# A two-layer attention and mixture-of-experts kernel on one core: next layer's tiles interleaved with a quarter's down weights, and the GpSimd share of the splits moved to ScalarE and VectorE

## The chip, the cores and the metric

The kernel runs on one core of a Trainium2 chip. The metric is the device time of one execution in microseconds (us). Engines are named as the profile names them: PE is TensorE, ACT is ScalarE, DVE is VectorE, POOL is GpSimd, SP is SyncE, whose queue here does nothing but issue transfers from HBM.

## What is computed

Two layers over 256 tokens of width 1024, then a last RMS norm. Each layer mixes the tokens in three ways (latent attention, stick-breaking attention with a soft plus, causal pooling), projects back, and adds a mixture of 32 experts with two experts chosen per token:

```python
def hybrid_layer(x, ...):
    hn = rms_norm(x, norm1_g)
    proj = jnp.einsum('bsd,df->bsf', hn, w_in)
    ya = mla_mixer(proj[..., :o1], proj[..., o1:o2], proj[..., o2:o3], ...)
    yb = stick_breaking_mixer(qkv_b[:, :, 0], qkv_b[:, :, 1], qkv_b[:, :, 2])
    yc = pool_mixer(proj[..., o4:], pool_w, pool_scale)
    x = x + jnp.einsum('bsm,md->bsd', jnp.concatenate([ya, yb, yc], -1), w_out)
    return x + hier_moe(rms_norm(x, norm2_g), ...)

# stick breaking: strict is the mask of earlier positions
log_1m_beta = jnp.where(strict, -jax.nn.softplus(z), 0.0)
between = lax.cumsum(log_1m_beta, axis=3, reverse=True) - log_1m_beta
a = jnp.where(strict, jnp.exp(jax.nn.log_sigmoid(z) + between), 0.0)

# experts
a, b = einsum('nd,edf->nef', t, w_gate[g]), einsum('nd,edf->nef', t, w_up[g])
y = y + einsum('nef,efd->nd', silu(a) * b * combine[:, g, :, None], w_down[g])
```

Everything is float32. The expert weights alone are some 200 MB, so the traffic from HBM is the larger part of the work.

## The kernel before, in words

**Storage.** `Ring` (L43) holds 25 slots of 1 MB in SBUF: 12 pairs and one single. All weights pass through them, in the fixed order of a list, `stream`, that `Net.__init__` fills (L229 to L259). A rehearsal of the program (`rehearsed`, L126) finds, for each entry of the list, the first moment in the program at which a slot is free. SP issues the transfers one after the other in the list's order; an issue waits until the last reader of its slot is done, and all that follow in the list wait behind it. Entries are named by tile: `wa`, `wqk`, `wvu` are the parts of the input projection (0.8 to 1 MB each, two of each per layer), `sm`, `uq`, `wo` are other mixer weights, `wh` are gate and up weights of the experts, `ww` and `wt` their down weights. `wt` holds the down weights of six of the eight expert groups, cut in four quarters of the output columns; one entry of 2 MB has a quarter's weights of two groups.

**Exact products in two parts.** The input projection, the latent projections and the output projection multiply each operand as a high part (rounded to the reduced format fp32r) and a low part (the rest), in three matmuls (`mm3`, L312). `parts` (L318) makes the two: the high part by a copy, the low part by a subtraction of it. `weights` (L327) lists the pieces of the mixer weights, each 128 x 512 or 128 x 416, and `split` (L348) makes the parts of the next piece into one of four buffers, four pieces ahead of PE. In the kernel before, a piece with an even number has its high part from ACT and its low part from DVE. A piece with an odd number has its high part from DVE (a cast) and its low part from POOL, unless its last argument `how` forbids it (the first quarter of layer 0, `sm` and `uq`). 38 pieces go the odd way. In the stick-breaking part, `stick_parts` (L590) makes the parts of the soft plus, 128 x 768 at a time, twice in each layer: high from ACT, low from POOL.

**Stages of a layer.** `mixers` (L523) runs the value projections (`values_in`), the attention scores `z` of the stick-breaking heads, the soft plus of them (Abs, Exp, Ln on ACT, L578 to L582, then L584 on DVE), the latents (`latents` L477, `rescale` L493), the query projection, and at L673 `breaks`, the last reader of the soft plus's parts `sH` and `sL`. `route` chooses experts. `experts` (L912) goes through eight groups, then through the four quarters of the output columns (L1016). In a quarter each of the six groups has: `down` (16 matmuls with `wt`), `parts` of the result (a copy on ACT, a subtraction on DVE), one step of the next layer's input projection (`next(beside)`, L1033), and `scatter` (4 matmuls back to the tokens). The steps beside the second quarter (q = 1) are two with `wa`, two with `wqk`, two with `wvu`, all of the next layer's first tiles; beside the first quarter there are none, since the new x is not yet there. `arrive` (L403) transposes the quarter of x that has just become final and makes its parts.

Each engine works in the order in which its instructions are written. The order around the change is thus the order of `stream` for SP, and the order of calls of `split`, `parts` and `stick_parts` for ACT, DVE and POOL.

Of the kernel before, what the change touches and what calls it, by code (L numbers as in the profile page):

```python
# [9 lines left out]
F32 = mybir.dt.float32  # L10
# [4 lines left out]
OP = mybir.AluOpType  # L15
AX = mybir.AxisListType

L, S, D = 2, 256, 1024
# [9 lines left out]
SM_UK, SM_UV, SM_PW, SM_RT = 0, 512, 1024, 1280  # L28
# [166 lines left out]
class Net:  # L195
    def __init__(self, tc, ctx, a, plan):
# [20 lines left out]
        def w(l, k, *idx, then=()):  # L217
            for i in idx:
                add(f"{k}{i}.{l}", a[k][l, i], *then)
# [13 lines left out]
        for l in range(L):  # L233
            w(l, "wvu", *range(min(l, 1), 2))
            add(f"sm.{l}", a["small"][l])
            add(f"uq.{l}", a["uq"][l])
            w(l, "wo", 3, 2, 0, 1)
            for g in range(8):
                for i in range(0, 12 if g < 8 - TAIL else 8, 2):
                    src = a["wh"][(l * 8 + g) * 4 + i // 2] if i < 8 else a["ww"][(l * (8 - TAIL) + g) * 2 + i // 2 - 4]  # L240
                    add(f"we{g * 12 + i}.{l} we{g * 12 + i + 1}.{l}", src)
            for q in range(4):
                if l + 1 == L:
                    if q == 1:
                        add("fg", a["fg"])
                elif q < 3:
                    w(l + 1, ("wa", "wqk", "wa")[q], q // 2)
                    if q == 1:
                        w(l + 1, "wvu", 0)
                else:  # L250
                    w(l + 1, "wqk", 1)
                for p in range(TAIL // 2):
                    names = [f"we{(8 - TAIL + 2 * p + i) * 12 + 8 + q}.{l}" for i in range(2)]
                    src = tails(l, q, p)
                    if (l, q, p) == (L - 1, 3, TAIL // 2 - 1):
                        for i in range(2):
                            add(names[i], src[:, i * 2048:i * 2048 + 2048])
                    else:
                        add(" ".join(names), src)  # L259

        c = lambda n, *s, dt=F32: cst.tile([128, *s], dt, name=n)
# [22 lines left out]
        for i, n in ((0, 4), (8, 32)):  # L284
            k = min(i, 4)
# [29 lines left out]
        self.mm(out, a[0], b[1], False, False)  # L315
        self.mm(out, a[1], b[0], False, stop)

    def parts(self, hi, lo, in_, scale=None, pool=False):  # L318

        V = self.nc.gpsimd if pool else self.nc.vector  # L320
        self.ev("v" if pool else "a", hi, in_, scale)
        if scale is None:
            V.tensor_tensor(lo, in_, hi.bitcast(F32), op=OP.subtract)  # L323
        else:
            V.scalar_tensor_tensor(lo, in_, scale, hi.bitcast(F32), op0=OP.mult, op1=OP.subtract)  # L325

    def weights(self, l):  # L327

        add = lambda name, c, n, last, how=0: self.feed.append((f"{name}.{l}", c, n, last, how))
        for q in range(4):  # L330
            for name, n in (("wa", 416), ("wqk", 512)):
                for k in (2 * q, 2 * q + 1):
                    add(f"{name}{k // 4}", k % 4 * n, n, k % 4 == 3, l + q == 0)
            for k in range(2 * q, 2 * q + 2) if l and q < 2 else ():
                add(f"wvu{k // 4}", k % 4 * 512, 512, k % 4 == 3)
        for k in range(4 if l else 0, 8):
            add(f"wvu{k // 4}", k % 4 * 512, 512, k % 4 == 3)
        add("sm", SM_UK, 512, False, 1)
        add("sm", SM_UV, 512, False, 1)
        for j in range(4):  # L340
            add("uq", j * 512, 512, j == 3, 1)
        for c in (6, 7, 4, 5, 0, 1, 2, 3):
            for n in range(2):
                add(f"wo{c // 2}", c % 2 * 1024 + n * 512, 512, c % 2 + n == 2)
        self.wbuf = [v3(t, 4, 512) for t in self.ring.two("wHL")]
        self.turns = 0

    def split(self, ahead=AHEAD):  # L348

        while self.feed and len(self.ready) <= ahead:  # L350
            name, c, n, last, how = self.feed.popleft()
            piece = self.ring.get(name)[:, c:c + n]
            hl = [b[:, self.turns % 4, 0:n] for b in self.wbuf]
            self.parts(*hl, piece, pool=self.turns % 2 and not how)
            self.turns += 1
            self.ready.append(hl)
            if last:
                self.ring.drop(name)
# [164 lines left out]
    def mixers(self, l):  # L523
        nc, ps, ring, vec = self.nc, self.ps, self.ring, self.vec
        sm, mm, mm3, ev, tr = self.sm, self.mm, self.mm3, self.ev, self.tr
        V, A, G = nc.vector, nc.scalar, nc.gpsimd
# [32 lines left out]
        sp, dT = v3(spare, 4, 384), v3(spare, 2, 256, 1536)  # L559
# [15 lines left out]
        for h in (0, 2):  # L575
            hs = slice(h, h + 2)
# [11 lines left out]
        sH, sL = (v3(t, 4, 384) for t in ring.two("sHL"))  # L588

        def stick_parts(h):  # L590
            hs = slice(h, h + 2)
            A.activation(sH[:, hs], sp[:, hs], AF.Copy)
            G.tensor_tensor(sL[:, hs], sp[:, hs], sH[:, hs].bitcast(F32), op=OP.subtract)

        for t in range(2):
            ev("av"[t], vu[:, t], ps[:, 6 + t], r1[:, t:t + 1])
# [2 lines left out]
        w = self.weight()  # L599
        for j in range(2):  # L600
            b = ps[:, 4 + j]
            for e in range(2):
                c = (2 * j + e) * 128
# [4 lines left out]
        w = self.weight()  # L608
# [633 lines left out]
```

## Time and profile before

| | us |
|---|---|
| median of 3 runs (609.23, 611.42, 611.27) | 611.27 |
| the profiled execution | 609.29 |
| its span | 607.7 |
| PE busy in the span | 525.3 (86%) |
| DVE, ACT, POOL busy | 255.2, 146.3, 93.5 |
| SP's transfers (227.33 MB), share of the 16 DMA engines' time | 91.2% |

The span runs from the first to the last instruction of the profiled execution, and 1.6 us of its time lie outside. Busy time is the union of the instructions of an engine. PE's is no measure of its peak, since matmuls overlap and their ends are modelled. The transfers are busy for most of the span, so the times at which they are not are the ones to look for.

### The profile page before, as it was taken

How to read it: one execution, taken by the hardware profiler on the slowest of the kernel's cores; microseconds unless marked ns; L12 is line 12 of the kernel's file. 1: busy time of each engine (PE TensorE's matmuls, PEld its weight loads, DVE VectorE, ACT ScalarE, POOL GpSimd, SP SyncE). 2: the span in 40 equal slices, each digit the busy share in tenths (PEclk: the TensorE clock that was granted, in tenths of full speed). 3: DMA queues.
4: the chain of work that ended last, by engine and by line, in shares of the span. 5: the costliest groups of instructions: out<-in, count | busy, mean ns of one | idle time of the engine just before them, and what ended most of it. 6: DMA issues, size and time to landing. Idle time of an engine off the chain costs nothing. (4 is left out here: it accounts for less than half of the span.)

```text
span 607.7 us, 10429 instructions
## 1 busy us (share of the span) xinstructions
PE 525.3 (86%) x4232; PEld 342.2 (56%) x4232; DVE 255.2 (42%) x640; ACT 146.3 (24%) x351; POOL 93.5 (15%) x138
## 2 busy tenths in 40 slices
PE   8989999898886887769997799998898578889983
PEld 7968877554341543446766597774254325435652
DVE  4879765432320222143337686663332212212322
ACT  4465543200000001122223844422000000012212
POOL 2534323000000000011212332310000000100001
PEclk9999999999997899879999899999999879998998
DMA  8999778999999999999999729879999999999992
GB/s 300 399 424 397 258 297 293 369 387 424 424 427 424 426 427 426 425 423 428 427 418 428 306 63 355 313 304 386 385 422 428 424 424 428 425 426 428 426 386 77
DMA packets 25407, 228.72 MB, mean 376 GB/s; under 512 B 2817, under 2 KB 5121, under 8 KB 6914
## 3 DMA queue, kind: packets, MB, share of 16 engines
q1 hardware_dynamic: 24914, 227.33, 91.2%
q8 instruction: 37, 0.61, 0.4%
q10 hardware_dynamic: 432, 0.59, 0.3%
q14 instruction: 24, 0.20, 0.1%
HBM read 226.85 MB, written 1.05 MB: 375 GB/s over the span
## 5 line engine op out<-in xcount | busy, mean ns | idle before, releaser
L305 PE MATMUL ps<-pair,pair 128*32 128x256 f32 (+7 forms) x3152 | 385.6, 440 | 56.1 <-DVE pair L893 20.2
L305 PEld LDWEIGHTS ps<-pair,pair 128*32 128x32 f32 (+2 forms) x3152 | 226.8, 143 | 181.6 <-issue 102.9
L305 PE MATMUL ps<-pair 128*128 128x256 f32 (+7 forms) x416 | 78.3, 364 | 4.6 <-DVE pair L893 3.5
L371 ACT ACTIVATE pair<-ps 128x256 fp32r<-128x256 f32 (+5 forms) x82 | 36.8, 451 | 147.2 <-PE ps L305 133.8
L305 PEld LDWEIGHTS ps<-pair 128*128 128x128 f32 (+3 forms) x416 | 49.8, 182 | 32.8 <-issue 15.8
L323 DVE TENSOR_TENSOR pair<-ps,pair 128x256 fp32r<-128x256 f32 (+1 forms) x58 | 25.1, 433 | 86.5 <-ACT pair L371 86.5
L323 POOL TENSOR_TENSOR pair<-pair,pair 128x512 fp32r<-128x512 f32 (+1 forms) x33 | 43.8, 1327 | 93.2 <-DVE pair L373 60.4
L946 DVE TENSOR_REDUCE ws<-ps 128x1 f32<-128x256 f32 x16 | 6.8, 425 | 121.8 <-PE ps L365 121.8
L943 ACT ACTIVATE pair<-ps 128x256 f32<-128x256 f32 x16 | 6.1, 384 | 207.4 <-PE ps L305 193.4
L323 DVE TENSOR_TENSOR pair<-pair,pair 128x512 fp32r<-128x512 f32 (+1 forms) x47 | 44.6, 951 | 14.4 <-ACT pair L371 13.8
L922 POOL TENSOR_TENSOR pair<-pair,comb 128x128 f32<-128x128 f32 x32 | 12.2, 401 | 235.6 <-PE ps L305 223.2
L906 DVE TENSOR_TENSOR pair<-ps,vec 128x512 f32<-128x512 f32 x32 | 22.1, 691 | 49.5 <-PE ps L305 49.3
L371 ACT ACTIVATE pair<-pair 128x512 fp32r<-128x512 f32 (+1 forms) x47 | 28.9, 619 | 15.2 <-PE ps L305 10.3
L365 PE MATMUL ps<-ident,pair 128*128 128x128 f32 x128 | 23.3, 286 | 5.0 <-DVE pair L948 2.9
L373 DVE COPY pair<-ps 128x512 f32<-128x512 f32 (+3 forms) x25 | 17.1, 689 | 23.7 <-PE ps L305 15.4
L365 PEld LDWEIGHTS ps<-ident,pair 128*128 128x128 f32 x128 | 14.4, 141 | 22.3 <-issue 13.8
L305 PE MATMUL ps<-ident,ones 128*128 128x128 f32 x140 | 23.9, 303 | 1.6 <-POOL ident L274 1.6
L305 PEld LDWEIGHTS ps<-ident,ones 128*128 128x128 f32 x140 | 20.2, 210 | 3.6 <-issue 2.0
L325 DVE SCALAR_TENSOR_TENSOR pair<-ps,vec,pair 128x256 fp32r<-128x256 f32 x26 | 12.4, 482 | 19.1 <-ACT pair L371 19.1
L371 ACT ACTIVATE pair<-ps,vec 128x256 fp32r<-128x256 f32 x26 | 12.1, 474 | 27.2 <-PE ps L365 12.2
L641 ACT ACTIVATE pair<-pair,low 128x128 f32<-128x128 f32 (+1 forms) x32 | 14.1, 446 | 9.3 <-DVE low L635 9.3
L323 POOL TENSOR_TENSOR pair<-one,pair 128x416 fp32r<-128x416 f32 (+1 forms) x5 | 6.1, 1217 | 55.6 <-DVE pair L373 55.6
(143 smaller groups left out, 333.9 us busy)
## 6 DMA issues: line engine op xcount, KB each, us to landing
pair<-in_wh SPq DMA_DIRECT2D x39, 2048.0 KB, 19.1
pair<-in_wh SPq DMA_DIRECT2D x47, 1024.0 KB, 11.2
pair<-in_wt SPq DMA_DIRECT2D x23, 2048.0 KB, 32.3
pair<-in_ww SPq DMA_DIRECT2D x11, 1024.0 KB, 7.4
pair<-in_wo SPq DMA_DIRECT2D x8, 1024.0 KB, 18.1
pair<-in_ww SPq DMA_DIRECT2D x2, 2048.0 KB, 8.1
pair<-in_wqk SPq DMA_DIRECT2D x3, 1024.0 KB, 33.5
pair<-in_wvu SPq DMA_DIRECT2D x3, 1024.0 KB, 11.5
```

The lines of the kernel that those rows point to most:

```text
L305: self.nc.tensor.matmul(out, lhsT, rhs, start=start, stop=stop, skip_group_check=True)
L323: V.tensor_tensor(lo, in_, hi.bitcast(F32), op=OP.subtract)
L325: V.scalar_tensor_tensor(lo, in_, scale, hi.bitcast(F32), op0=OP.mult, op1=OP.subtract)
L365: self.nc.tensor.transpose(out, in_, self.ident)
L371: nc.scalar.activation(out, in_, AF.Copy, scale=1.0 if scale is None else scale)
L373: nc.vector.tensor_copy(out, in_)
L641: A.activation(s[:, c], s[:, c], AF.Exp, scale=-1.0, bias=low[:, h, j:j + 1], accum_out=sums[:, h, j:j + 1])
L906: self.nc.vector.tensor_tensor(xs[:, 4 * n:4 * n + 4], v3(self.ps[:, b0 + n], 4, 128), self.vec[:, l, 8 + 4 * n:12 + 4 * n, None].to_broad ...
L922: G.tensor_tensor(d4, d4, comb[:, t, 4 * g:4 * g + 4, None].to_broadcast([128, 4, 32]), op=OP.mult)
L943: A.activation(h, ps[:, 2, 0:256], AF.Silu)
L946: V.tensor_reduce(ws, ps[:, 3, 256:512], axis=AX.X, op=OP.add)
```

## The change

In layer 0's tail, the second quarter's entries of the stream stood as `wqk0`, `wvu0`, `wt`, `wt`, `wt`. They now stand as `wt`, `wqk0`, `wt`, `wvu0`, `wt`. And POOL makes no parts any more: of all pieces of weights, and of the soft plus, ACT makes the high part and DVE the low part.

```diff
@@ -244,12 +244,13 @@
                 elif q < 3:
-                    w(l + 1, ("wa", "wqk", "wa")[q], q // 2)
-                    if q == 1:
-                        w(l + 1, "wvu", 0)
+                    if q != 1:
+                        w(l + 1, "wa", q // 2)
                 else:
                     w(l + 1, "wqk", 1)
                 for p in range(TAIL // 2):
+                    if l + 1 < L and q == 1 and p:
+                        w(l + 1, ("wqk", "wvu")[p - 1], 0)
                     names = [f"we{(8 - TAIL + 2 * p + i) * 12 + 8 + q}.{l}" for i in range(2)]
@@ -315,10 +316,10 @@
-    def parts(self, hi, lo, in_, scale=None, pool=False):
+    def parts(self, hi, lo, in_, scale=None):
 
-        V = self.nc.gpsimd if pool else self.nc.vector
-        self.ev("v" if pool else "a", hi, in_, scale)
+        V = self.nc.vector
+        self.ev("a", hi, in_, scale)
@@ -348,10 +349,10 @@
             hl = [b[:, self.turns % 4, 0:n] for b in self.wbuf]
-            self.parts(*hl, piece, pool=self.turns % 2 and not how)
+            self.parts(*hl, piece)
@@ -590,7 +591,7 @@
             A.activation(sH[:, hs], sp[:, hs], AF.Copy)
-            G.tensor_tensor(sL[:, hs], sp[:, hs], sH[:, hs].bitcast(F32), op=OP.subtract)
+            V.tensor_tensor(sL[:, hs], sp[:, hs], sH[:, hs].bitcast(F32), op=OP.subtract)
```

The rest of the diff takes the argument `how` out of `weights`. The new code has one line more from L247 on, so its L324 is the old L323.

SP's queue at the second quarter of layer 0's tail, before (a number behind `pair` tells the tile):

```order
L93 DMA pair_95<-in_wqk 128x2048
L93 DMA pair_971<-in_wvu 128x2048
L75 DMA pair_121<-in_wt 128x4096
L75 DMA pair_123<-in_wt 128x4096
L75 DMA pair_125<-in_wt 128x4096
L93 DMA pair_95<-in_wa 128x1664
```

and now:

```order
L75 DMA pair_971<-in_wt 128x4096
L93 DMA pair_95<-in_wqk 128x2048
L75 DMA pair_123<-in_wt 128x4096
L93 DMA pair_121<-in_wvu 128x2048
L75 DMA pair_125<-in_wt 128x4096
L93 DMA pair_95<-in_wa 128x1664
```

The same 8 MB, with the first 2 MB of down weights moved ahead of the two tiles; two of the tiles have changed places in the ring. No other row of SP's queue changes its order.

ACT at the same place, from the parts of the quarter of x that has arrived (`pair_2450`) on; `pair_1315` are the parts of a group's result, `pair_2451` the parts of weights. Before:

```order
L371 ACTIVATE pair_2450<-ps,vec 128x256
L380 ACTIVATE pair_127,ss<-x 128x256
L371 ACTIVATE pair_1315<-ps 128x256
L371 ACTIVATE pair_2451<-pair_95 128x512
L371 ACTIVATE pair_1315<-ps 128x256
L371 ACTIVATE pair_2451<-pair_971 128x512
L371 ACTIVATE pair_1315<-ps 128x256 x2
```

and now:

```order
L372 ACTIVATE pair_2450<-ps,vec 128x256
L381 ACTIVATE pair_127,ss<-x 128x256
L372 ACTIVATE pair_1315<-ps 128x256
L372 ACTIVATE pair_2451<-one 128x416
L372 ACTIVATE pair_2451<-pair_95 128x512 x2
L372 ACTIVATE pair_1315<-ps 128x256
L372 ACTIVATE pair_2451<-pair_121 128x512
L372 ACTIVATE pair_1315<-ps 128x256
L372 ACTIVATE pair_2451<-pair_121 128x512
L372 ACTIVATE pair_1315<-ps 128x256
```

Every piece now has its high part here, so the first piece of `wvu0` (`pair_121`) stands between the parts of the second and the third group's results, as it did before, and the second one behind the third's.

DVE in layer 0, from the evacuation of the projections (L375) to the query projection's (L620); `pair_149` are the parts of weights. Before:

```order
L375 TENSOR_SCALAR pair_95<-ps,r_320 128x512
L323 TENSOR_TENSOR pair_149<-pair_113,pair_149 128x512
L373 COPY pair_95<-ps 64x2x256 x2
L323 TENSOR_TENSOR pair_149<-pair_113,pair_149 128x512
L373 COPY pair_95<-ps 128x512
L323 TENSOR_TENSOR pair_149<-pair_113,pair_149 128x512
L620 TENSOR_TENSOR pair_110<-ps,tq 128x512
L323 TENSOR_TENSOR pair_149<-pair_113,pair_149 128x512
L620 TENSOR_TENSOR pair_110<-ps,tq 128x512
L373 CAST pair_149<-pair_113 128x512
L620 TENSOR_TENSOR pair_110<-ps,tq 128x512
```

and now:

```order
L376 TENSOR_SCALAR pair_95<-ps,r_320 128x512
L324 TENSOR_TENSOR pair_149<-pair_113,pair_149 128x512
L374 COPY pair_95<-ps 64x2x256 x2
L594 TENSOR_TENSOR pair_148<-pair_119,pair_148 128x768
L324 TENSOR_TENSOR pair_149<-pair_113,pair_149 128x512
L374 COPY pair_95<-ps 128x512
L324 TENSOR_TENSOR pair_149<-pair_113,pair_149 128x512
L621 TENSOR_TENSOR pair_110<-ps,tq 128x512
L324 TENSOR_TENSOR pair_149<-pair_113,pair_149 128x512
L621 TENSOR_TENSOR pair_110<-ps,tq 128x512
L594 TENSOR_TENSOR pair_148<-pair_119,pair_148 128x768
L324 TENSOR_TENSOR pair_149<-pair_113,pair_149 128x512
```

The two subtractions of the soft plus (L594) have come to DVE, and a cast has become a subtraction.

## Rows read from the trace of the kernel before

**Rows 1.** Busy time by stretches: stretch, its length, engines, PEclk, DMA share, GB/s.

```profile
54.00:64.00 10.00, 9.30 (x85) 8.80 (x84) 9.62 (x22) 3.25 (x11) 3.13 (x2) 1.00 0.57 239
260.00:270.00 10.00, 5.59 (x44) 3.55 (x45) 4.38 (x9) 2.40 (x8) 1.82 (x2) 0.66 1.00 427
347.00:360.60 13.60, 13.60 (x109) 12.85 (x109) 12.92 (x26) 6.76 (x16) 5.07 (x4) 0.91 0.00 0
398.00:594.00 196.00, 170.63 (x1543) 94.81 (x1546) 56.42 (x151) 22.63 (x52) 10.73 (x26) 0.96 0.98 408
```

**Rows 2.** SP's waits, 0 to 130 us, then 330 to 412: total, times, longest.

```profile
SPq L75 <- PE ps L305: 67.1, 12, 31.4
...
SPq L75 <- PE ps L305: 56.8, 8, 33.7
```

**Rows 3.** Timeline of SP's issues: start, length, what was issued.

```profile
63.88 4.86 SPq L75 DMA_DIRECT2D pair<-in_ww  x3
...
360.59 0.81 SPq L75 DMA_DIRECT2D pair<-in_ww  x2
```

**Rows 4.** Timeline of PE, 255 to 366 us; in brackets idle time before and its releaser.

```profile
258.84 0.66 PE L365 MATMUL ps<-ident,x 128*128 128x128 f32 x4 [0.84 <-DVE x L1045]
264.41 3.88 PE L305 MATMUL ps<-pair,pair 128*32 128x256 f32 x22 [4.92 <-DMA pair<-in_wt]
...
268.68 2.40 PE L305 MATMUL ps<-pair,pair 128*32 128x256 f32 x22
...
274.01 0.64 PE L305 MATMUL ps<-pair 128*128 128x256 f32 x4
...
345.53 9.16 PE L305 MATMUL ps<-pair,pair 128*128 128x512 f32 x54 [3.86 <-ACT pair L371]
```

**Rows 5.** Timeline of SP, the third `wt` entry of the second quarter.

```profile
239.13 0.33 SPq L75 DMA_DIRECT2D pair<-in_wt  x1
```

**Rows 6.** DMA issues of 239.0 to 239.5 us: KB, us from issue to landing.

```profile
pair<-in_wt SPq DMA_DIRECT2D x1, 2048.0 KB, 35.0
```

**Rows 7.** Timeline of PE in layer 0, 33 to 57 us.

```profile
33.32 1.23 PE L365 MATMUL ps<-ident,pair 128*128 128x128 f32 x8 [1.17 <-DVE pair L503]
...
42.20 0.50 PE L305 MATMUL ps<-pair,pair 128*128 128x512 f32 x1 [0.45 <-DVE pair L373]
43.93 11.88 PE L305 MATMUL ps<-pair,pair 128*128 128x512 f32 x73 [1.23 <-POOL pair L323]
56.50 2.77 PE L305 MATMUL ps<-pair,pair 128*128 128x256 f32 x18 [0.70 <-DVE pair L323]
```

**Rows 8.** Timelines of DVE and POOL at places where both work.

```profile
30.80 1.25 DVE L496 TENSOR_TENSOR s<-s,r 128x4 f32<-128x4 f32 x1 [0.38 <-POOL s L487]
...
30.73 1.30 POOL L323 TENSOR_TENSOR pair<-pair,pair 128x512 fp32r<-128x512 f32 x1
...
325.19 0.16 DVE L433 TENSOR_TENSOR rr<-rr,widths 128x4 f32<-128x4 f32 x1
...
351.99 2.13 DVE L323 TENSOR_TENSOR pair<-pair,pair 128x512 fp32r<-128x512 f32 x1
...
351.73 1.85 POOL L593 TENSOR_TENSOR pair<-one,pair 128x768 fp32r<-128x768 f32 x1 [2.12 <-ACT pair L592]
...
44.83 0.89 DVE L323 TENSOR_TENSOR pair<-pair,pair 128x512 fp32r<-128x512 f32 x1
```

**Rows 9.** Timelines of ACT and DVE in layer 0, 37 to 48 us.

```profile
37.62 0.84 ACT L371 ACTIVATE pair<-ps,vec 128x256 fp32r<-128x256 f32 x2 [3.23 <-POOL pair L323]
...
41.30 0.62 ACT L371 ACTIVATE pair<-pair 128x512 fp32r<-128x512 f32 x1
...
47.71 0.69 ACT L371 ACTIVATE pair<-ps,r 128x512 f32<-128x512 f32 x1 [0.33 <-PE ps L305]
...
41.74 0.41 DVE L373 CAST pair<-pair 128x512 fp32r<-128x512 f32 x1
42.07 0.68 DVE L323 TENSOR_TENSOR pair<-pair,pair 128x512 fp32r<-128x512 f32 x1
```

More of the change, by code (lines that the diff above doesn't have):

```diff
@@ L327, in weights @@
     def weights(self, l):
-        add = lambda name, c, n, last, how=0: self.feed.append((f"{name}.{l}", c, n, last, how))
+        add = lambda name, c, n, last: self.feed.append((f"{name}.{l}", c, n, last))
         for q in range(4):
@@ L332, in weights @@
                 for k in (2 * q, 2 * q + 1):
-                    add(f"{name}{k // 4}", k % 4 * n, n, k % 4 == 3, l + q == 0)
+                    add(f"{name}{k // 4}", k % 4 * n, n, k % 4 == 3)
             for k in range(2 * q, 2 * q + 2) if l and q < 2 else ():
@@ L337, in weights @@
             add(f"wvu{k // 4}", k % 4 * 512, 512, k % 4 == 3)
-        add("sm", SM_UK, 512, False, 1)
-        add("sm", SM_UV, 512, False, 1)
+        add("sm", SM_UK, 512, False)
+        add("sm", SM_UV, 512, False)
         for j in range(4):
-            add("uq", j * 512, 512, j == 3, 1)
+            add("uq", j * 512, 512, j == 3)
         for c in (6, 7, 4, 5, 0, 1, 2, 3):
@@ L350, in split @@
         while self.feed and len(self.ready) <= ahead:
-            name, c, n, last, how = self.feed.popleft()
+            name, c, n, last = self.feed.popleft()
             piece = self.ring.get(name)[:, c:c + n]
             hl = [b[:, self.turns % 4, 0:n] for b in self.wbuf]
-            self.parts(*hl, piece, pool=self.turns % 2 and not how)
+            self.parts(*hl, piece)
             self.turns += 1
```

## The prediction, made before the changed kernel was run

> **What bounds the kernel now.** I first read the busy time by stretches [rows 1]. From 398 to 594 us the transfers are busy for 0.98 of the time at 408 GB/s, so the end is set by the moment at which this last run of transfers starts. Between 347.0 and 360.6 us they move nothing, and PE is busy throughout; from 54 to 64 us, at the same place in layer 0, they run at 239 GB/s. SP's waits say why [rows 2]: its longest waits in both layers, 31.4 and 33.7 us, are ended by PE matmuls. The issues that end them, at 63.88 and 360.59 [rows 3], are of `ww` entries whose slots held the soft plus's parts, and the last matmuls that read those are the ones of `breaks`. So the ring is full, transfers stop, and they go on when PE has come to the end of `breaks`. How much is loaded before each hole is fixed by the ring and by the order of `stream`. Whatever lets PE reach `breaks` earlier in layer 0 or layer 1 makes the hole shorter and moves everything behind it; the two gains add up.
>
> What makes PE late? In layer 1 the row at 264.41 shows it [rows 4]: the quarter before is done with its transposes at 258.84 + 0.66 = 259.5, and the second quarter's first group waits 4.92 us for its down weights. From there to 322 us PE runs almost without idle time; the two later quarters start on weights that have landed. So these 4.92 us are carried to the hole. In the ten microseconds around it the granted clock is 0.66 in the mean [rows 1], so part of it was at 1.2 GHz, and the first group took 3.88 us where the second took 2.40 [rows 4]. Later there is a wait of 3.86 us at 345.53 for ACT. In layer 0 PE waits 1.17, 0.45, 1.23 and 0.70 us between 33 and 57 us [rows 7]: for DVE, for a cast, for POOL's subtraction and for DVE's.
>
> **The change, part by part.**
>
> *The order of the stream.* It removes no transfer; 8 MB in the same place are issued in another order. The third `wt` entry is last in both orders. It lands at 239.13 + 35.0 = 274.1 us [rows 5, 6]. At 427 GB/s [rows 1] 2 MB take 4.9 us and 1 MB 2.5 us. Counted back in the old order, the first `wt` lands at 274.1 - 9.8 = 264.3, which is when PE's wait ended. In the new order `wvu0` lands at 269.2, the second `wt` at 266.7, `wqk0` at 261.8 and the first `wt` at 259.3. PE is ready at 259.5, so the wait of 4.92 us goes. Issues are no limit, since they are some 30 us ahead of their landing. On SP nothing else moves.
>
> What is late next: pieces of weights are split four ahead, so the first piece of `wvu0` stands on ACT between the results of the second and the third group. ACT stands there until 269.2, and the third group's result, whose matmuls need the second `wt` (266.7), is behind it. Its parts come after a high part of 0.62 us [rows 9], and take an estimated 0.8 us themselves (half as wide as the 0.62 and 0.68 of rows 9, one after the other). So its `scatter` starts at about 270.7, against 274.01 before [rows 4]. From there PE goes on as before. Gain 3.2 us. The bounds are 0, if the new wait eats all of it, and 4.9 + 1.5 = 6.4 us, if `wvu0` holds up nobody and the first group runs at the full clock (3.88 against 2.40). I take 3.2, since the landing time of `wvu0` is bound to the order of the queue.
>
> *No parts on POOL.* 38 pieces lose a cast on DVE (0.41 us) and a subtraction on POOL, and gain a copy on ACT (0.62) and a subtraction on DVE (0.68) [rows 9]. Over the whole program this puts 38 x 0.62 = 24 us on ACT and 38 x 0.27 = 10 us on DVE, mostly beside PE that is bound by itself. What counts is the path to `breaks`.
>
> First, the latents. At 30.80 DVE needs 1.25 us for a product of 128 x 4 numbers while POOL subtracts; the same size takes 0.16 where POOL does nothing [rows 8]. So 1.1 us vanish on the way to the transposes for which PE waited 1.17 us [rows 7]. Layer 1 has the same two instructions at the same place: 1.1 us there too, carried through ACT's chain to the wait at 345.53, because that chain is started by PE's next matmuls.
>
> Second, layer 0's values. PE waited 0.45 for a cast and 1.23 for POOL's subtraction behind it, then 0.70 for a DVE subtraction that ran long [rows 7]. Cast and subtraction now take 0.62 + 0.68. With the latents this could give 1.1 + 0.45 + 1.23 + 0.70 = 3.5 us. Against it stands ACT: from 37.62 to 47.71 it has hardly any idle time, 0.33 us of it at the end [rows 9], and two more high parts, 1.24 us, come into that chain. Its start is helped, because it was held up by POOL's subtraction [rows 9]. I take 3.5 - 1.2 = 2.3 us, between -0.1 (1.1 - 1.24, where ACT sets the pace) and 3.5. In layer 1 the pieces in that chain are of the kind that ACT made before as well, so nothing is added there.
>
> *The soft plus's low part.* Four subtractions of 128 x 768 move from POOL (1.85 us) to DVE. DVE's price is not in the trace; the bounds are 0.68, that of 512 columns, and POOL's 1.85 [rows 8, 9]. I take 1.0, in proportion to the columns. DVE is nearly full there (9.62 of 10 us, 12.92 of 13.60 [rows 1]), but its own subtractions get shorter: the one at 351.99 takes 2.13 us beside POOL's, while 0.68 is the length without [rows 8, 9]. Two such per layer pay for the two that come. I take zero.
>
> The sum is 3.2 + 1.1 + 2.3 = 6.6 us: 609.29 becomes 602.7 for the profiled execution. The median of the runs lies 2.0 us above that execution, so I forecast 611.27 - 6.6 = **604.7 us**. A measurement of this kernel can tell about 0.5% (3.1 us) from no change.
>
> **The rivals.**
>
> *All waits go* (chance 0.13): the order gives 6.4, layer 0 3.5, latents 1.1; 11.0 us, 600.3. For it speaks that PE has little other idle time; against it that `wvu0` cannot land before 269.2.
>
> *The new wait eats the order's gain* (0.10): ACT stands at `wvu0`, and all parts behind it come so late that PE is where it was at 274. Then 3.4 us remain, 607.9. Against it: `wvu0` lands 4.8 us before that.
>
> *ACT sets the pace* (0.08): its high parts delay the evacuations in layer 0 (gain -0.1) and by one high part the latents of layer 1 (1.1 - 0.6 = 0.5), so that 3.2 - 0.1 + 0.5 = 3.6 us remain, 607.7. For it speaks the full ACT stretch [rows 9]. The cast that moves takes 0.41 us on DVE and 0.62 on ACT. The Trainium skill (Perfetto Trace Analysis, Optimizing Scalar/DVE Operations) says of work that either engine can do that with a DVE performance mode "it will be faster" there; by that rule the casts belong where they were, and the trace's two lengths agree with it.
>
> *DVE becomes the engine that PE waits for* (0.06), between the evacuations and `breaks`. If the subtractions stay long without POOL's next to them (0.89 at 44.83 [rows 8], which has only a masking of POOL beside it) and those of 768 columns take 1.85, layer 0 gets 2 x 1.85 + 3 x (0.89 - 0.41) = 5.1 us and layer 1 3.7 + 0.5 = 4.2, less the idle 0.4 and 0.7 [rows 1]: 8.2 us later, the latents' gains lost, the order's 3.2 kept. That is 5.0 us slower, 616.3; it turns to the slow side as soon as more than 3.2 of the 8.2 us arise. Against it stands the 0.68 us of rows 9. The Trainium skill (SBUF — State Buffer, Who interferes with whom) says that a DVE instruction with two inputs in SBUF contends with a POOL one that reads SBUF, and that the second fully blocks. By that rule POOL's masks, which stay, go on blocking DVE; the trace shows 0.2 us for it at 44.83 and 1.4 beside a subtraction.
>
> *Nothing moves* (0.03): PE is held by something that the trace does not name, 611.3.
>
> **How the numbers follow.** My forecast has a chance of 0.60, with 602.3 to 607.0 as its own range (ACT's 1.2 us back or not, 1 us either way in the order). The range for 8 in 10 goes from 600.0 to 609.5: it takes in the first three rivals, and leaves out the last two and what lies beyond the first. Faster by over 0.5%, below 608.2: 0.60 + 0.13 and half of the second and third rivals, 0.82. Slower, above 614.3: 0.06. Within: 0.12.
>
> **What would show it.** In the profile after, PE's wait for `wt` near 264 should be below 1 us and a wait for DVE of about 1 us should stand before the third group's `scatter`; the 128 x 4 product should take 0.2 us in both layers; DVE subtractions of 512 columns should stay near 0.7 us and those of 768 at about 1.0; the stretch without transfers should end 2 us earlier in layer 0 and over 6 us earlier in layer 1; the last run of transfers should be as long as now. I am wrong if PE's wait comes back with ACT or DVE as its releaser, or if the hole ends earlier and the end does not.

## The result and the profile after

| | before | the change |
|---|---|---|
| median, beside each other (4 runs each) | 610.25 us (608.93 to 611.42) | **603.27 us** (602.82 to 604.39) |
| ratio, 95% interval | | 0.9889 [0.9859, 0.9919] |
| the profiled execution, its span | 609.29, 607.7 | 603.47, 601.8 |
| DVE, ACT, POOL busy | 255.2, 146.3, 93.5 | 251.2, 165.9, 36.6 |

The forecast was 604.7 us, and the change came to -7.0 us where -6.6 was forecast. The medians from here on leave out three runs that were 14 to 26% longer at a granted clock of 0.65 to 0.73. Line numbers are one higher in the kernel after: L306 is the old L305, and so on.

Busy time of the change by stretches, which answer to [rows 1]:

```profile
54.00:60.70 6.70, 6.70 (x65) 6.44 (x64) 5.70 (x18) 2.57 (x9) 0.45 (x1) 1.00 0.82 342
260.00:270.00 10.00, 7.56 (x66) 5.63 (x64) 4.17 (x10) 3.90 (x10) 0.00 (x0) 1.00 1.01 427
341.90:355.50 13.60, 13.60 (x109) 12.84 (x110) 11.92 (x28) 7.51 (x18) 0.77 (x2) 0.91 0.13 55
393.00:589.00 196.00, 169.76 (x1550) 94.62 (x1550) 56.49 (x151) 22.83 (x53) 10.69 (x26) 0.97 0.98 408
```

The last run of transfers is as long as before and as dense (0.98, 408 GB/s); it starts earlier. In the ten microseconds of the second quarter PE is busy for 7.56 us where it had 5.59, and the granted clock is 1.00 in place of 0.66. The holes end earlier, as the timeline of SP shows beside [rows 3]: 3.2 us in layer 0, 5.1 us in layer 1.

```profile
60.67 0.80 SPq L75 DMA_DIRECT2D pair<-in_ww  x2
...
355.46 0.80 SPq L75 DMA_DIRECT2D pair<-in_ww  x2
```

PE in the second quarter, for [rows 4]; under it ACT at the same place:

```profile
258.69 2.40 PE L306 MATMUL ps<-pair,pair 128*32 128x256 f32 x22 [0.41 <-DMA pair<-in_wt]
260.92 0.65 PE L306 MATMUL ps<-pair 128*128 128x256 f32 x4
261.50 2.40 PE L306 MATMUL ps<-pair,pair 128*32 128x256 f32 x22
...
265.92 2.69 PE L306 MATMUL ps<-pair,pair 128*32 128x256 f32 x28 [1.55 <-DMA pair<-in_wt]
269.40 0.50 PE L306 MATMUL ps<-pair 128*128 128x256 f32 x2 [0.79 <-ACT pair L372]
270.19 0.51 PE L306 MATMUL ps<-pair 128*128 128x256 f32 x2 [0.29 <-DVE pair L324]
```

```profile
268.44 0.63 ACT L372 ACTIVATE pair<-pair 128x512 fp32r<-128x512 f32 x1 [5.42 <-DMA pair<-in_wvu]
268.98 0.37 ACT L372 ACTIVATE pair<-ps 128x256 fp32r<-128x256 f32 x1
```

The wait of 4.92 us is 0.41 now, and the first group takes 2.40 us, not 3.88. ACT stands for `wvu0` for 5.42 us, and only then copies the third group's result (268.98); that group's `scatter` waits 0.79 and 0.29 us for it. This is the queue that the prediction described. The wait of 1.55 us for the second `wt` it had not named; it costs nothing, since the third group's result would stand behind `wvu0` anyhow (in e1 below it is 0.59 us long, and the quarter ends as long after the last landing).

DVE's lines for [rows 8, 9], and PE's in layer 0 for [rows 7]:

```profile
29.17 0.16 DVE L497 TENSOR_TENSOR s<-s,r 128x4 f32<-128x4 f32 x1
...
49.36 0.96 DVE L594 TENSOR_TENSOR pair<-pair,pair 128x768 fp32r<-128x768 f32 x1
50.23 0.69 DVE L324 TENSOR_TENSOR pair<-pair,pair 128x512 fp32r<-128x512 f32 x1
```

```profile
30.61 1.23 PE L366 MATMUL ps<-ident,pair 128*128 128x128 f32 x8
...
39.62 3.01 PE L306 MATMUL ps<-pair,pair 128*128 128x512 f32 x12 [0.36 <-DVE pair L324]
43.08 2.86 PE L306 MATMUL ps<-pair,pair 128*128 128x512 f32 x17 [0.45 <-DVE pair L324]
46.23 0.96 PE L306 MATMUL ps<-pair,pair 128*128 128x512 f32 x3 [0.29 <-ACT pair L372]
47.45 0.96 PE L306 MATMUL ps<-pair,pair 128*128 128x512 f32 x3 [0.26 <-DVE pair L376]
48.77 7.33 PE L306 MATMUL ps<-pair,pair 128*128 128x256 f32 x56 [0.36 <-DVE pair L374]
```

The product of 128 x 4 takes 0.16 us (in layer 1 too, at 325.02), the transposes wait for nobody, the soft plus's subtraction takes 0.96 us (estimate: 1.0), the one beside it 0.69. But in place of the three waits behind them, of 0.45, 1.23 and 0.70 us, there are five of 0.26 to 0.45.

**Where the time came from, stretch by stretch.** A difference of two whole profiles mixes the change with what differs between any two executions. So I cut PE's timeline at events which no such difference shifts against each other, and did the same for every kernel of the experiments below. All numbers are differences of two starts of PE rows, in us; D is one row's length, and E starts at the landing of the second quarter's last `wt` (its issue plus the time to landing, as in [rows 5, 6]: 274.16 before, 273.26 in the change). E ends at these rows of PE, before and in the change:

```profile
284.70 0.66 PE L365 MATMUL ps<-ident,x 128*128 128x128 f32 x4 [0.84 <-DVE x L1045]
...
280.74 0.66 PE L366 MATMUL ps<-ident,x 128*128 128x128 f32 x4 [0.84 <-DVE x L1046]
```

The stretches are:

- A: input projection of layer 0, from the transposes of x's second quarter to the matmuls with `ones`
- B, F: from there to the transposes of the latents, in layers 0 and 1
- C, G: from there to the first matmul with `nones` in `breaks`, in layers 0 and 1
- D: the 32 matmuls of the second expert group's gather in layer 0
- E: from the landing to the transposes of the quarter of x that becomes final

| kernel | A | B | C | D | E | F | G |
|---|---|---|---|---|---|---|---|
| before | 20.36 | 3.17 | 25.96 | 4.10 | 10.5 | 2.99 | 24.52 |
| the change | 19.68 | 1.92 | 25.51 | 5.72 | 7.5 | 1.93 | 24.45 |
| e1 order alone | 20.36 | 3.15 | 25.94 | 5.72 | 7.5 | 2.98 | 24.15 |
| e2 parts alone | 19.66 | 1.90 | 25.49 | 5.72 | 10.5 | 1.91 | 25.03 |
| e3 two on POOL | 19.68 | 3.00 | 25.54 | 5.72 | 7.5 | 1.91 | 24.43 |
| e4 soft plus on POOL | 19.60 | 1.91 | 25.48 | 4.10 | 7.5 | 1.91 | 24.41 |
| e5 casts on DVE | 19.60 | 2.18 | 24.45 | 4.10 | 7.5 | 2.18 | 24.43 |
| e6 `wvu0` last | 19.70 | 1.91 | 25.48 | 4.09 | 17.3 | 1.91 | 24.70 |
| e7 piece later | 19.70 | 1.91 | 25.47 | 5.72 | 7.1 | 1.93 | 24.80 |
| e8 values out early | 19.66 | 1.90 | 25.48 | 5.72 | 7.5 | 1.91 | 22.81 |
| e11 the change again | 19.66 | 1.91 | 25.47 | 5.72 | 7.5 | 1.91 | 24.83 |
| e10 PE kept busy | 19.66 | 1.91 | 25.47 | 4.10 | 7.5 | 1.93 | 24.56 |
| e9 together | 19.70 | 2.18 | 24.46 | 4.09 | 7.1 | 1.91 | 22.05 |
| e12 together, PE busy | 19.66 | 2.18 | 24.46 | 4.09 | 7.1 | 1.91 | 23.63 |

From before to the change: A -0.68, B -1.25, C -0.45, E -3.06 (10.54 to 7.48), F -1.06, in all **-6.5 us**; the medians differ by 7.0. Column for column the stretches repeat within 0.1 us between kernels that are alike there; only D and G do not. D has just two values; G is 24.45 and 24.83 in two executions of the changed kernel (the change and e11), so a difference of 0.4 us in G says nothing.

A to G end at `breaks`, and the end of the program follows. From the issue that ends the second hole to the end of the span it is 246.4 to 247.1 us in 13 of the 14 profiles, and 248.3 in e8's, whose second expert group in layer 1 has the 5.72 us of D.

### The profile page after: what moved, and what is told of

It reads as the page before. It is cut to its first block, busy times and chain, and to the rows that moved or that the text cites. A ratio compares the mean times of both kernels' runs of the same rounds, so it can differ in the third digit from the quotient of the medians.

```text
span 601.8 us, 10392 instructions
## 1 busy us (share of the span) xinstructions
PE 524.5 (87%) x4232; PEld 343.0 (57%) x4232; DVE 251.2 (42%) x644; ACT 165.9 (28%) x389; POOL 36.6 (6%) x96
## 5 line engine op out<-in xcount | busy, mean ns | idle before, releaser
L306 PE MATMUL ps<-pair,pair 128*32 128x256 f32 (+7 forms) x3152 | 383.0, 438 | 52.2 <-DVE pair L894 19.8
L306 PEld LDWEIGHTS ps<-pair,pair 128*32 128x32 f32 (+2 forms) x3152 | 225.8, 142 | 175.6 <-issue 100.4
L306 PE MATMUL ps<-pair 128*128 128x256 f32 (+7 forms) x416 | 80.6, 371 | 5.7 <-DVE pair L894 3.5
L306 PEld LDWEIGHTS ps<-pair 128*128 128x128 f32 (+3 forms) x416 | 51.7, 187 | 34.7 <-issue 16.2
L324 DVE TENSOR_TENSOR pair<-pair,pair 128x512 fp32r<-128x512 f32 (+1 forms) x80 | 53.4, 679 | 21.1 <-ACT pair L372 19.8
L324 DVE TENSOR_TENSOR pair<-ps,pair 128x256 fp32r<-128x256 f32 (+1 forms) x58 | 25.1, 433 | 76.8 <-ACT pair L372 76.7
L372 ACT ACTIVATE pair<-pair 128x512 fp32r<-128x512 f32 (+1 forms) x80 | 48.6, 619 | 15.8 <-PE ps L306 8.4
L306 PE MATMUL ps<-ident,ones 128*128 128x128 f32 x140 | 23.4, 299 | 1.6 <-POOL ident L275 1.6
L306 PEld LDWEIGHTS ps<-ident,ones 128*128 128x128 f32 x140 | 19.8, 207 | 3.6 <-issue 1.6
L326 DVE SCALAR_TENSOR_TENSOR pair<-ps,vec,pair 128x256 fp32r<-128x256 f32 x26 | 12.4, 483 | 18.5 <-ACT pair L372 18.5
L366 PE MATMUL ps<-ident,x 128*128 128x128 f32 x64 | 10.2, 289 | 3.9 <-DVE x L1046 3.4
L381 ACT ACTIVATE pair<-x 128x256 f32<-128x256 f32 (+1 forms) x20 | 10.0, 499 | 10.7 <-DVE x L1046 6.3
## 6 DMA issues: line engine op xcount, KB each, us to landing
pair<-in_wh SPq DMA_DIRECT2D x39, 2048.0 KB, 19.6
```

Source lines behind the costliest of these rows:

```text
L306: self.nc.tensor.matmul(out, lhsT, rhs, start=start, stop=stop, skip_group_check=True)
L366: self.nc.tensor.transpose(out, in_, self.ident)
L372: nc.scalar.activation(out, in_, AF.Copy, scale=1.0 if scale is None else scale)
L381: self.nc.scalar.activation(junk, in_, AF.Square, accum_out=acc)
```

## The experiments

All are made from the changed kernel except e1, and each was timed beside the kernel before (its median was 610.11 for e1 to e4, 609.95 for e5 to e8, 609.78 for the rest).

**e1 and e2: one half of the change each.** e1 is the kernel before with the stream's part of the diff, e2 the changed kernel without it.

> The kernel before with the new order of the stream alone; POOL keeps its parts. Theory (three places add up: order 2.9 us, latents 1.1 us a layer, the rest of layer 0): 607.2 us, 3.0 below the 610.25 of before; the issue of ww after layer 0's hole stays at 63.9, PE's wait for wt at 264 falls below 1 us, and the issue of ww after layer 1's hole moves from 360.6 to 357.6. Rival A (the whole gain is POOL's going): 610.2 and an issue at 360.6. Rival B (the whole gain is the order's): 603.3 and an issue at 355.5.

> The changed kernel with the old order of the stream; POOL makes no parts. Theory: 606.3 us, 4.0 below before; issue of ww in layer 0 at 60.7, the wait of 4.9 us for wt in the second quarter is there as before, issue of ww in layer 1 at 358.4 (1.1 for layer 1's latents, some 1.1 of layer 0's 3.2). Rival A (all of it is POOL's going): 603.3 and 355.5. Rival B (all is the order): 610.2 and 360.6.

e1: 607.10 us (12 runs), ratio 0.9941 [0.9910, 0.9972]. e2: 607.24 us (12 runs), ratio 0.9947 [0.9924, 0.9971]. So -3.0 and -2.9 us: neither half is the whole, and together they give 5.9 of the 7.0, which the intervals allow (by the ratios, 0.59 and 0.53% against 1.11). e1 came out as expected, e2 0.9 us above. The second hole ended at 358.59 and 359.10, 1.0 and 0.7 us later than expected; both profiles have a D of 5.72, to which e10 comes back. In the table, D and G aside, e1 has only E in common with the change, and e2 all but E. Their first group of the second quarter, PE's timeline of e2 and then of e1:

```profile
263.51 3.86 PE L305 MATMUL ps<-pair,pair 128*32 128x256 f32 x22 [4.36 <-DMA pair<-in_wt]
```

```profile
261.53 2.71 PE L306 MATMUL ps<-pair,pair 128*32 128x256 f32 x22
...
268.28 2.69 PE L306 MATMUL ps<-pair,pair 128*32 128x256 f32 x28 [0.59 <-DMA pair<-in_wt]
271.74 0.50 PE L306 MATMUL ps<-pair 128*128 128x256 f32 x2 [0.77 <-ACT pair L372]
```

The old order keeps the wait and the slow first group, whoever makes the parts. The new order removes both, and ACT's 0.77 us come in their place.

**e3: what POOL cost the latents.**

```diff
-            self.parts(*hl, piece)
+            self.parts(*hl, piece, pool=self.turns == (17, 19)[int(name[-1])])
```

`pool` puts that piece's subtraction on POOL; the argument's way through `parts` is left out here.

> The changed kernel with two subtractions back on POOL, one in each layer: the piece that POOL subtracted beside the latents' 128 x 4 product. Nobody needs that piece for several us. Theory (what POOL costs is that a DVE instruction beside it runs longer): the product takes 1.25 us in both layers where it took 0.16, the transposes behind it wait for DVE about 1 us, the holes end 1.1 (layer 0) and 1.1 to 2.2 us (layer 1) later, 604.4 to 605.5 us. Rival (it was the wait for POOL's result): nobody waits, the product stays at 0.16, 603.3 us.

603.84 us (6 runs), ratio 0.9886 [0.9850, 0.9922]. DVE, POOL and PE of e3 in layer 0:

```profile
29.85 1.25 DVE L497 TENSOR_TENSOR s<-s,r 128x4 f32<-128x4 f32 x1 [0.71 <-POOL s L488]
```

```profile
29.79 1.30 POOL L324 TENSOR_TENSOR pair<-pair,pair 128x512 fp32r<-128x512 f32 x1
```

```profile
32.38 0.79 PE L366 MATMUL ps<-ident,pair 128*128 128x128 f32 x4 [1.01 <-DVE pair L504]
```

One subtraction on POOL, for whose result nobody waits, makes the product of 128 x 4 eight times as long and B 1.08 us longer. So it is the overlap that costs, not a wait for POOL. In layer 1 my expectation missed: the piece that I chose is not the one beside the product, the product took 0.16 us there, and F stayed at 1.91. The miss serves as a control: POOL's subtraction at 322.59 lengthened another product of 128 x 4 (L434, 1.29 us from 322.61 on, 0.17 in the change), for which PE does not wait. The Trainium skill (SBUF — State Buffer, Who interferes with whom) says that a DVE instruction with two inputs in SBUF contends with a POOL instruction that reads SBUF; the 1.25 against 0.16 us agree. The median moved by 0.6 us only, less than the interval can tell; the 1.08 us are shown in the stretch.

**e4: the soft plus's subtractions back on POOL.**

```diff
-            V.tensor_tensor(sL[:, hs], sp[:, hs], sH[:, hs].bitcast(F32), op=OP.subtract)
+            G.tensor_tensor(sL[:, hs], sp[:, hs], sH[:, hs].bitcast(F32), op=OP.subtract)
```

> The changed kernel with the soft plus's four subtractions back on POOL. Theory of the prediction (what DVE saves, four times 0.95 us, it loses again, since its own subtractions beside POOL's take 2.1 us where they took 0.68): 603.3 us, within 0.5; one or two DVE subtractions a layer of 1.5 to 2.2 us, issues of ww at 60.7 and 355.5 within 0.5. Rival A (DVE is full there, so 0.95 us twice a layer are given back to PE): holes end up to 1.9 us earlier each, 600.5. Rival B (the lengthened subtractions hold up the scores): holes end 1 us later each, 605.

602.46 us (5 runs), ratio 0.9865 [0.9824, 0.9905]. DVE and POOL of e4, layer 0:

```profile
49.95 1.51 DVE L324 TENSOR_TENSOR pair<-pair,pair 128x512 fp32r<-128x512 f32 x1
52.10 0.68 DVE L324 TENSOR_TENSOR pair<-pair,pair 128x512 fp32r<-128x512 f32 x1
53.30 1.74 DVE L324 TENSOR_TENSOR pair<-pair,pair 128x512 fp32r<-128x512 f32 x1
```

```profile
49.07 1.84 POOL L594 TENSOR_TENSOR pair<-pair,pair 128x768 fp32r<-128x768 f32 x1 [1.48 <-PE ps L306]
52.43 2.06 POOL L594 TENSOR_TENSOR pair<-pair,pair 128x768 fp32r<-128x768 f32 x1 [1.52 <-ACT pair L593]
```

DVE saves 2 x 0.96 us and its two subtractions beside POOL's are (1.51 - 0.68) + (1.74 - 0.68) = 1.9 us longer. C and G are the change's within 0.04 us: this part of the change is worth nothing, as forecast (in layer 1 this is known to 0.4 us only, the scatter of G). The median is 0.8 us below the change's, but no stretch that the edit touches is shorter; its profiled execution had a D of 4.10, the change's 5.72 (see e10).

**e5: the odd pieces' high parts cast on DVE.**

```diff
-            self.parts(*hl, piece)
+            odd = self.turns % 2 and not (name[:2] in ("sm", "uq") or name[-1] == "0" and self.turns < 4)
+            self.parts(*hl, piece, high="v" if odd else "a")
```

`high` names the engine of the high part.

> The changed kernel with the high part of the 38 odd pieces cast on DVE again (0.41 us) in place of a copy on ACT (0.62 us); DVE makes the low parts of all. POOL makes none. Theory (in the stretches that count DVE is as full as ACT, so what ACT saves DVE loses): 603.3 us within 1; layer 0's waits for DVE grow by 0.4 or less each, those for ACT shrink. Rival, by the Trainium skill (Perfetto Trace Analysis, Optimizing Scalar/DVE Operations: work that either engine can do is faster on DVE where it has a performance mode): ACT paces layer 0, its holes end 1.2 us earlier (two copies of 0.62), 602. Rival B (DVE sets the pace): each of the three pieces in layer 0's chain costs 0.41 us, 604.5.

602.04 us (6 runs), ratio 0.9873 [0.9837, 0.9909]. PE of e5:

```profile
40.11 0.51 PE L306 MATMUL ps<-pair,pair 128*128 128x512 f32 x1 [0.38 <-DVE pair L375]
40.83 7.24 PE L306 MATMUL ps<-pair,pair 128*128 128x512 f32 x35 [0.22 <-DVE pair L324]
48.43 7.33 PE L306 MATMUL ps<-pair,pair 128*128 128x256 f32 x56 [0.36 <-DVE pair L375]
```

C is 1.06 us shorter: three waits in place of five. So my expectation was wrong and the rival by which ACT paces layer 0 right: the copies on ACT did hold layer 0's values, by nearly the 1.24 us of the prediction's term. But B and F are 0.27 us longer each, since a cast now stands on DVE ahead of the latents. So the cast, 0.41 us on DVE and 0.62 on ACT [rows 9], belongs on DVE in the one stretch where ACT is the later engine, and not in the two where DVE is. The Trainium skill (Perfetto Trace Analysis, Optimizing Scalar/DVE Operations) says of work that either engine can do that it is faster on DVE where a DVE performance mode is available, and that a saturated DVE is a reason to move some of it; the two lengths agree with the first half, and B and F fit the second.

**e6 and e7: the place of `wvu0`.** e6 moves `wvu0` behind the last `wt` of the quarter. e7 leaves the stream and splits one piece less ahead at the quarter's second step:

```diff
-        ps, w, k = self.ps, self.weight(AHEAD - (q == 1 and part == 3)), 2 * q + part % 2
+        ps, w, k = self.ps, self.weight(AHEAD - (q == 1 and part == 3 or l == 1 and q == 0 and part == 1)), 2 * q + part % 2
```

> The changed kernel with wvu0 behind the third wt entry: wt, wqk0, wt, wt, wvu0. No down weight comes later than in the change, the third one 2.5 us earlier. Theory (ACT stands at the first piece of wvu0, and the third group's result is queued behind it): the third group's scatter comes 4.9 us later than in the change, after the landing of wvu0; the second quarter ends 12.4 us after that landing where the change's ends 7.48 us after the landing of the last wt; 608.0 us. Rival (only the down weights' landing counts): the second quarter ends up to 2.5 us earlier than in the change, 601 to 603.3.

> The changed kernel, but the pieces of weights are split only three ahead at the second step of the second quarter, so that the first piece of wvu0 stands behind the third group's result on ACT. Theory (the transfers are the next limit): the waits of 0.79 (ACT) and 0.29 us (DVE) before the third scatter go, and a wait of some 0.6 us for the third wt entry takes their place at the fifth group; the second quarter ends 7.0 us after that entry's landing in place of 7.48; 602.8 us. Rival (PE gets all of it): 1.1 us, 602.2, and no wait for wt there.

e6: 609.74 us (11 runs), ratio 0.9994 [0.9973, 1.0015]: the whole gain of the change is gone, though every down weight lands as early as in the change or earlier. PE of e6, and its busy time by stretches:

```profile
273.98 1.58 PE L308 MATMUL ps<-pair 128*128 128x256 f32 x4 [5.67 <-ACT pair L374]
275.49 4.78 PE L308 MATMUL ps<-pair,pair 128*32 128x256 f32 x28
```

```profile
268.30:274.00 5.70, 0.03 (x2) 0.02 (x1) 0.31 (x1) 0.97 (x3) 0.00 (x0) 0.94 1.04 436
274.00:280.00 6.00, 6.00 (x32) 4.22 (x33) 2.33 (x5) 1.27 (x3) 0.00 (x0) 0.50 1.01 428
```

PE stands 5.67 us for ACT, which stands for `wvu0`, as ACT's row of e6 says:

```profile
273.02 0.63 ACT L374 ACTIVATE pair<-pair 128x512 fp32r<-128x512 f32 x1 [10.33 <-DMA pair<-in_wvu]
```

The quarter ends 14.8 us after the landing of `wvu0`, where I expected 12.4: after the wait the granted clock is 0.50, the lower of PE's levels, for 6 us, and the next rows take 1.58 and 4.78 us where the change has 2 x 0.5 and 2.69. The queue on ACT is shown; its price was too low, because the clock behind a wait was not in it.

e7: 603.90 us (6 runs), ratio 0.9886 [0.9852, 0.9919]. PE of e7:

```profile
269.30 0.64 PE L306 MATMUL ps<-pair 128*128 128x256 f32 x4
...
274.16 2.65 PE L306 MATMUL ps<-pair,pair 128*32 128x256 f32 x22 [1.12 <-DMA pair<-in_wt]
```

The third `scatter` waits for nobody, and later in the quarter PE waits 1.12 us for the last `wt` (0.6 was expected). E falls by 0.42 (7.06), as expected; the median, expected at 602.8, does not show it. So with the new order the transfers themselves set the second quarter, and 0.4 us was all that ACT's queue still cost there.

**e8: the other wait in layer 1.** PE waits 3.88 us at 340.52 in the change, as it did before [rows 4]. The edit is an order alone: in layer 1 the calls that evacuate the values stand before the first soft plus's Exp, those of the latent keys before the second's Abs.

```diff
         for h in (0, 2):
...
+            if l and h:
+                latent_keys()
             A.activation(sp[:, hs], zb[:, hs, 0:384], AF.Abs)
...
+            if l and not h:
+                values_in(len(blocks))
+                evacuate()
```

> The changed kernel with another order in layer 1 alone: the values' two evacuations before the first soft plus's Exp, the latent keys' matmuls and evacuations before the second soft plus's Abs; no work is added or removed. In the change PE waits 3.88 us at 340.52 for ACT, which has the values' evacuation behind the second Abs, Exp and Ln (2.5 us). Theory: the wait goes, and the next limit is the latent values' evacuation, so layer 1's hole ends 2.0 to 2.7 us earlier, 601.0 us. Rival A (all of the 3.88 us): 599.4. Rival B (the soft plus, now 1.7 us later on ACT, holds up breaks): 603.3 or more.

602.37 us (6 runs), ratio 0.9853 [0.9816, 0.9889]. G is 1.64 us shorter than the change's and 2.02 than e11's (22.81), where 2.0 to 2.7 was expected; the median of 601.0 was not reached. PE's wait is this one:

```profile
340.59 7.50 PE L306 MATMUL ps<-pair,pair 128*128 128x256 f32 x48 [2.13 <-DVE pair L374]
```

It is DVE's evacuation of the latent keys, which stands behind the first soft plus's sum on DVE.

**e10 and e11: why the profile of the change shows only 5.1 us at the second hole.** e11 is the changed kernel again; e10 adds, before the second expert group's gather in each layer,

```diff
+            if g == 1:
+                self.warm(8, 7)
```

> The changed kernel once more, beside the next three. Theory (what its profiled execution lost behind the first expert group was the clock of that execution, 32 matmuls in 5.72 us where the profile of before had 4.10): 603.3 us in the median, executions between 601.8 and 604.4 with two levels some 1.6 us apart. Rival (the change itself makes that stretch longer): 603.3 with all executions within 0.6 us, and the 5.72 us again.

> The changed kernel with eight matmuls of ones added in each layer, into a PSUM bank that nobody reads, in PE's idle time of 2.1 us before the second expert group's gather. Theory (PE's idle time there lets the clock fall to its lower level in some executions, which costs 1.6 us, in layer 0 and in layer 1): the granted clock is 1.00 there, the 32 matmuls take 4.1 us in both layers, executions lie within 1 us of each other, the median is 602.0. Rival A (the clock falls there whatever PE does in those 2 us): 5.72 us in some profiles, median and spread as in the change. Rival B (the added matmuls hold up the gather): 0.5 us later in each layer, 604.

e11: 603.83 us (603.38 to 605.07, 6 runs), ratio 0.9894 [0.9866, 0.9922]; its executions make no two clear levels. e10: 603.16 us (601.46 to 603.56, 6 runs), ratio 0.9878 [0.9849, 0.9907]; 602.0 within 1 us was expected. PE at that place, before, in the change and in e10 (where the trace counts 16 matmuls for the eight of the program):

```profile
121.32 4.10 PE L305 MATMUL ps<-pair 128*128 128x128 f32 x32 [1.72 <-DVE pair L893]
```

```profile
115.97 0.44 PE L366 MATMUL ps<-ident,pair 128*128 128x128 f32 x2
118.13 5.72 PE L306 MATMUL ps<-pair 128*128 128x128 f32 x32 [1.73 <-DVE pair L894]
```

```profile
117.06 1.95 PE L306 MATMUL ps<-ident,ones 128*128 128x128 f32 x16
118.95 4.10 PE L306 MATMUL ps<-pair 128*128 128x128 f32 x32
```

Of the 12 profiles without the added matmuls, before and the change among them, seven have 5.72 us there (granted clock 0.70 in the change's) and five 4.10; before happened to be one of the five. Of the same gather in layer 1, one of twelve has 5.72 (e8). So the 1.6 us belong to the execution and not to the change, and where the clock fell, PE had idled 1.73 us just before; but it had idled as long ahead of the rows of 4.10. With PE kept busy all four have 4.09 or 4.10. Four are too few to show that the matmuls did it, and the median of e10, 0.7 us below e11's, lies within the intervals: neither is shown.

That D is what the second hole lacks, the profiles do show. From the end of the first hole to that of the second it is 296.7 us before, 294.6 to 295.1 in the change, e3, e7 and e11, which have a D of 5.72, and 292.6 and 292.8 in e4 and e10, which have before's 4.10. The last two are 4.1 and 3.9 us shorter than before, and E and F together make 4.1.

**e9 and e12: what helped, together.** e9 has e5's casts for layer 0's value weights alone, e7's lookahead, and e8 with the latent values also ahead of the second soft plus; e12 has e10's matmuls too.

> The changed kernel with what the experiments showed to help: the odd pieces of layer 0's value weights cast on DVE (its stretch from the transposes to breaks was 1.04 us shorter so), the first piece of wvu0 behind the third group's result (0.4 us), and in layer 1 the values' and both latents' evacuations ahead of the second soft plus (the order of which a first form gave 1.64 us, with 2.13 us of a wait for DVE left). Theory: the wait left in layer 1 goes too, and DVE's queue of evacuations is the next limit; layer 1's stretch from the transposes to breaks is 3.0 to 4.0 us shorter than the change's 24.45; in all 4.5 to 5.4 us, 598.3 us. Rival (DVE sets the pace at once): the stretch is 1.6 us shorter, 600.2.

> The version before with the eight idle matmuls a layer as well. Theory: 1.0 to 1.6 us below that version, 597.0 us, executions within 1 us. Rival (the clock does not hang on those 2 us): the same as that version, 598.3.

e9: 601.10 us (598.65 to 602.75, 6 runs), ratio 0.9848 [0.9816, 0.9880], above the 598.3 that I expected and the rival's 600.2. G is 22.05, 2.4 us below the change's, where 3.0 to 4.0 was expected. PE of e9 in layer 1:

```profile
336.84 4.58 PE L306 MATMUL ps<-pair,pair 128*128 128x256 f32 x36 [0.36 <-DVE pair L374]
342.42 0.50 PE L306 MATMUL ps<-pair,pair 128*128 128x256 f32 x2 [1.00 <-ACT pair L372]
343.90 1.46 PE L306 MATMUL ps<-pair,pair 128*128 128x256 f32 x10 [0.98 <-DVE pair L324]
```

The wait of 3.88 us is down to 0.36, and 1.00 and 0.98 us come later, for the parts of the last query weights, which now stand behind the second soft plus. B is 0.27 us longer, as in e5: the cast of a value weight stands ahead of the latents.

e12: **599.77 us** (599.57 to 599.85 in five of 6 runs, and 601.91), ratio 0.9832 [0.9803, 0.9861]: 4.1 us below the changed kernel in the same comparison, and below both kernels of this study, but 2.8 us above the 597.0 expected. Its profile has a G of 23.63, since the clock fell there: the rows behind the same two waits take 2.14 us where e9 has 1.46, and 2.41 where it has 1.48. Busy time of e12 by stretches:

```profile
342.00:347.00 5.00, 4.12 (x19) 3.92 (x19) 5.00 (x9) 1.89 (x3) 0.28 (x1) 0.66 0.08 31
```

## Why the prediction was right, point by point

- **What bounds the kernel.** Right. The last run of transfers kept its length, and what PE won ahead of `breaks` moved it. A to C lie ahead of the first hole, E to G ahead of the second, and e1 and e2, each with a part of them, gave its share at the end. From the second hole on all kernels but e8 take the same time within 0.7 us.
- **The order of the stream, 3.2 us.** 3.06 in E, 3.0 in e1's median (the two starts in the prediction, 274.01 and 270.7, give 3.3). The mechanism is the one described: ACT stands for `wvu0` with the third result behind it (268.44 and 268.98). e6 shows how much hangs on that queue. The upper bound of 6.4 us could not have been had: e7 frees the queue and the last `wt` gives back only 0.4.
- **The latents, 1.1 us a layer.** 1.25 and 1.06. e3 shows the cause with one instruction.
- **Layer 0, 2.3 us with the latents.** A, B and C together give 2.4, but not by the steps named. The three waits for cast, POOL and DVE were put at 2.38 less 1.24 for ACT, 1.1 us; C shows 0.45, and e5 gets 1.06 more from the same stretch by relieving ACT. So the high parts on ACT cost there about as much as I took them for, and the waits that went gave less. The 0.68 us of A make up for it, and that is luck. I had not looked at the input projection: before, six of POOL's subtractions ran there, three of DVE's beside them took 1.51 to 1.56 us (0.59 to 0.69 in the change), and PE waited 0.28 us for POOL at 15.12. That A goes with POOL's parts is shown (e2 has it, e1 has not); which of these rows makes it was not tried.
- **The soft plus, zero.** e4: 0.03 and 0.04 us.
- **The load on ACT and DVE.** ACT was to get 24 us and got 19.6. DVE was to get 10 and, with the soft plus, 4 more; it is 4.0 us less busy. The difference of 18 us is, by estimate, what DVE's own instructions had taken longer beside POOL; the forecast had counted that at the latents and the soft plus alone.
- **Two readings of [rows 8].** The product at 325.19 was read as one beside an idle POOL, and the subtraction at 44.83 as one beside a mask alone. These rows of POOL before show otherwise:

```profile
45.15 1.73 POOL L323 TENSOR_TENSOR pair<-pair,pair 128x512 fp32r<-128x512 f32 x1
...
325.22 1.30 POOL L323 TENSOR_TENSOR pair<-pair,pair 128x512 fp32r<-128x512 f32 x1 [1.51 <-PE ps L305]
```

The product began 0.03 us before POOL did. That it takes 0.16 beside an idle POOL is shown by the change, at 29.17 and 325.02. And the 0.2 us at 44.83 cannot be put down to the mask: in the change, a subtraction at 337.89 takes 0.68 us beside a mask that runs from 337.58 to 338.84.
- **The signs to look for.** The product at 0.16, the subtractions at 0.69 and 0.96, the wait near 264 below 1 us: right. The 1 us before the third `scatter` came as 0.79 for ACT and 0.29 for DVE. The holes were to end 2 us earlier and over 6: the rows say 3.2 and 5.1. In layer 0, 0.78 of it is the transfer of x, whose transposes start at 9.01 in place of 9.79 in that execution. In layer 1 the 1.6 us of D are missing, and some 0.6 us more that no stretch here accounts for. Two single profiles told these two rows less well than the stretches did.
- **The rivals.** ACT sets the pace: in C it does in part (e5), and that is why C gave 0.45. DVE becomes the engine that PE waits for: four of the five small waits, no loss. The wait that eats the order's gain: not here, but e6 is that rival, made by another order of the same five entries.

## What to carry to other kernels

An entry of a prefetch queue has two dates, that of its landing and that of the instruction that first waits for it on an in-order engine: order the queue by what stands *behind* that instruction too. A helper engine that shares the work of a busy one is worth what it takes over, less the time by which the busy one's own instructions get longer beside it, and the short ones on the critical chain pay most. Before a difference of two profiles is explained, cut both at common events and compare the stretches over several kernels; what varies among kernels that are alike there belongs to the execution.

## What was not expected of the hardware

A wait of PE can cost more than its length. After 5.67 us of idle time in e6 the granted clock was 0.50 for the next 6 us, and the next rows lost (1.58 - 2 x 0.5) + (4.78 - 2.69) = 2.7 us on top. In the kernel before, the first group behind the wait of 4.92 us took 3.88 us and not 2.40 [rows 4]. Even 1.73 us of idle time between two bursts is followed by the lower level in some executions of the same code (32 matmuls in 5.72 or 4.10 us), and with eight matmuls that compute nothing in that time the 32 took 4.09 or 4.10 us in all four cases seen, too few to show that it helps.

And a product of 512 numbers on DVE took 1.25 us, as long as POOL's subtraction of 65,536 beside it (1.30).
